# Gate-table products of a hybrid decoder step: the low part and the gate matching moved from GpSimd to VectorE

## The chip, the cores and the metric

One core of one Trainium2 chip runs one launch of the kernel. The metric is the device time of that launch in microseconds (us), the median of three runs. Engines are named as in the profile: PE is TensorE (PEld its weight loads), DVE is VectorE, ACT is ScalarE, POOL is GpSimd, SP issues most of the DMAs.

## What is computed

One decoder layer for 1024 prompt positions and 8 x 4 sample positions, 1056 columns in all. A token mixer (RWKV7 heads beside a pooling path) is followed by PEER, a lookup of 8 heads x 16 experts out of 16,384 per token, and by a gated embedding. The change lies in PEER:

```python
q = (xb @ wq).reshape(PEER_BLOCK, PEER_HEADS, 2, PEER_DK_HALF)
s1 = jnp.einsum('thc,nc->thn', q[:, :, 0], sub_keys[0])
s2 = jnp.einsum('thc,nc->thn', q[:, :, 1], sub_keys[1])
v1, i1 = lax.top_k(s1, PEER_TOPK)
v2, i2 = lax.top_k(s2, PEER_TOPK)
cand = (v1[..., :, None] + v2[..., None, :]).reshape(PEER_BLOCK, PEER_HEADS, PEER_TOPK * PEER_TOPK)
sc, ci = lax.top_k(cand, PEER_TOPK)
e1 = jnp.take_along_axis(i1, ci // PEER_TOPK, axis=-1)
e2 = jnp.take_along_axis(i2, ci % PEER_TOPK, axis=-1)
expert = e1 * N_KEYS + e2
gate = jax.nn.softmax(sc.astype(jnp.float32), axis=-1)
ue = jnp.take(u_tab, expert, axis=0)
act = jax.nn.gelu(jnp.einsum('thkd,td->thk', ue, xb).astype(jnp.float32), approximate=False) * gate
ve = jnp.take(v_tab, expert, axis=0)
return jnp.einsum('thk,thkd->td', act.astype(xb.dtype), ve)
```

## The kernel before

The 1056 columns are split in two. The last 384 gather their experts' rows (POOL's indirect DMAs). The first 672 are dense: every one of the 16,384 experts is computed for every column (U product, GELU, times a gate table, V product), and a table with one gate for each expert and column makes the unchosen ones zero. These tables are what the change touches.

The program has three stretches. First come the mixer's projections and most of the RWKV chunks. In the second, `phase_c` projects one group of 256 or 288 columns (W_out, then the queries) on PE, with weights that SP loads block by block (`whi`, `wlo` from `wc_d`), while `b_stream` runs the last RWKV chunks (small products at L470, with steps `ltm`, `lts`, `yx`, `yo` on POOL) and `t_stream` selects experts and builds gate tables for the group before. In the third, `dense` runs the expert products (L1118) on PE, block after block, and the gathers go on beside it.

The selection (`top`, `select`) takes the best 16 of each half and of their sums with DVE's eight-wide maximum, index and replace operations. Gates and codes come out in different orders, so they are matched: for two heads at a time `oh` is a 16 x 16 comparison of positions (L851, 512 columns), it is multiplied by the gates (L852), and summed along the row (L856). This is done four times for a tile of 128 columns, and once for the tile of 32 columns, which lies on the partitions as four sets of two heads.

The gate table of a token is a product of one-hot matrices over its 128 (head, rank) pairs, which lie on the partitions: row e1, column e2, weighted by the gate. The gate is split in two fp16 parts, high and low, in `e16` (fields 0 to 3 are e1, e2, the high part, the low part). For eight tokens at a time, in tile `ab` (fp16, two buffers), 84 times in all:

- L901 on DVE compares an iota with e1 and e2: two one-hot blocks, 2048 columns;
- L902 on DVE multiplies e2's block by the high part into a third block, 1024 columns;
- L904 multiplies e2's own block in place by the low part, in two halves of 512 columns. `GLO(t)` chooses the engine: POOL, unless t is a multiple of 12, which sends one half in three to DVE. The POOL operation goes through the helper `PTT`, so the profile shows it under L127;
- L912 on PE multiplies, for each token, the high block and the low block with e1's block (16 matmuls of 128 x 128), and ACT at L913 copies four tokens at a time to `gst`. Each 32 tokens are written to `g_d` by a DMA.

No table or cost of the program's author sets the order: the generators are merged by their share of steps, and the program's builder then schedules each engine's list by its own estimate. Each engine runs its list in order.

Of the kernel before, what the change touches and what calls it, by code (L numbers as in the profile page):

```python
# [16 lines left out]
ALU = mybir.AluOpType  # L17
# [30 lines left out]
GT8 = 8  # L48
SH = 4
NTC = ND // TC  # L50
EB = 128
# [12 lines left out]
def body(ctx, tc, io):  # L64
    nc = tc.nc
    mm = nc.tensor.matmul
    TT, STT, TS, ACT = (nc.vector.tensor_tensor, nc.vector.scalar_tensor_tensor, nc.vector.tensor_scalar,
                        nc.scalar.activation)
# [17 lines left out]
    def v3(ap, n):  # L86
        return ap.rearrange("p (a b) -> p a b", b=n)
# [38 lines left out]
    def PTT(out, a, b, op):  # L126
        nc.gpsimd.tensor_tensor(out, a, b, op=op)  # L127

    def PS(tag):
        return pools[tag].tile([128, 512], F32, name="ps", tag="bc" if tag in ("b0", "b1") else tag)  # L130
# [614 lines left out]
    def top(tk, pos, mt):  # L745
        src = sc_d[TIDX[pos]]
        if mt > TC:
            m, nh, loads = mt, HEADS, [(slice(0, mt), 0)]
        else:
            m, nh = mt * SH, HEADS // SH  # L750
            loads = [(slice(g * mt, (g + 1) * mt), 2 * nh * g) for g in range(SH)]
        V12 = tk.tile([128, HEADS, 2, TOPK], F32, name="V12", bufs=1)
        I12 = tk.tile([128, HEADS, 2, TOPK], U32, name="I12", bufs=1)
        for i in range(2 * nh):
            if i % 4 == 0:
                sq = tk.tile([128, 4, 128], F32, name="scq", bufs=2)
                for d, j in loads:
                    nc.sync.dma_start(sq[d], src[:mt, j + i:j + i + 4, :])
            s_ = sq[:m, i % 4, :]
            v8, i8 = V12[:m, i // 2, i % 2, :], I12[:m, i // 2, i % 2, :]  # L760
            nc.vector.max(v8[:, 0:8], s_)
            nc.vector.max_index(i8[:, 0:8], v8[:, 0:8], s_)
            s2 = tk.tile([128, 128], F32, name="s2", bufs=2)
            nc.vector.match_replace(s2[:m], v8[:, 0:8], s_, -BIG)
            nc.vector.max(v8[:, 8:16], s2[:m])
            nc.vector.max_index(i8[:, 8:16], v8[:, 8:16], s2[:m])
            yield
        yield from select(tk, pos, mt, m, nh, V12, I12)


    def select(tk, col, mt, m, nh, V12, I12):
# [7 lines left out]
        def pairs(src, dst, add):  # L779
            off = 0  # L780
            for a, b, w in SEG:
                k = b - a
                o = dst[:m, :nh, off:off + k * w]
                s1, s2_ = src[:m, :nh, 0, a:b], src[:m, :nh, 1, 0:w]
                if k == 1:
                    s1 = s1.to_broadcast([m, nh, w])
                elif w == 1:
                    s2_ = s2_.to_broadcast([m, nh, k])
                else:
                    o = o.rearrange("p h (k w) -> p h k w", w=w)  # L790
                    s1 = s1[:, :, :, None].to_broadcast([m, nh, k, w])
                    s2_ = s2_[:, :, None, :].to_broadcast([m, nh, k, w])
                add(o, s1, s2_, op=ALU.add)
                off += k * w
# [37 lines left out]
        gt = tk.tile([128, HEADS, TOPK], F32, name="gt")  # L832
# [15 lines left out]
        for h0 in range(0, nh, hb):  # L848
            hs, sh = slice(h0, h0 + hb), [m, hb, TOPK, TOPK]
            oh = tk.tile([128, hb, TOPK, TOPK], F32, name="oh", bufs=2)  # L850
            TT(oh[:m], cF[:m, hs, :, None].to_broadcast(sh), CF[:m, hs, None, :].to_broadcast(sh), op=ALU.is_equal)  # L851
            PTT(oh[:m], oh[:m], gt[:m, hs, None, :].to_broadcast(sh), op=ALU.mult)  # L852
            ohs.append((hs, oh))
            yield
        for hs, oh in ohs:
# [26 lines left out]
        m = mt  # L882
        nq = m // GT8
        e16 = gp.tile([128, 128 // GT8, 4, GT8], F16, name="e16")
# [5 lines left out]
        for t1 in range(0, m, TC):  # L890
            st = gp.tile([128, EB, TC], F32, name="gst", bufs=2)
            for t2 in range(0, TC, GT8):
                t = t1 + t2
                nb = GT8 // 2
                ab = gp.tile([128, 3 * nb, EB, 2], F16, name="ab", bufs=2)

                def pairs(j, n):
                    e = e16[:, t // GT8, j:j + n].rearrange("p j (a b) -> p (j a) b", b=2)
                    return e[:, :, None, :].to_broadcast([128, n * nb, EB, 2])

                TT(ab[:, 0:2 * nb], iota16[:, None, :, :].to_broadcast([128, 2 * nb, EB, 2]), pairs(0, 2), op=ALU.is_equal)  # L901
                TT(ab[:, 2 * nb:], ab[:, nb:2 * nb], pairs(2, 1), op=ALU.mult)  # L902
                for q in range(2):
                    GLO(t + 4 * q)(ab[:, nb + 2 * q:nb + 2 * q + 2], ab[:, nb + 2 * q:nb + 2 * q + 2],  # L904
                                   e16[:, t // GT8, 3:4, 4 * q:4 * q + 4].rearrange("p j (a b) -> p (j a) b", b=2)[:, :, None, :]
                                   .to_broadcast([128, 2, EB, 2]), op=ALU.mult)
                for q in range(0, GT8, 4):
                    ps = PS("b3")
                    for i in range(4):
                        a, o = divmod(q + i, 2)  # L910
                        for k in (2 * nb, nb):
                            mm(ps[:, i * 128:(i + 1) * 128], ab[:, k + a, :, o], ab[:, a, :, o], start=k > nb, stop=k == nb)  # L912
                    ACT(st[:, :, t2 + q:t2 + q + 4].rearrange("p e t -> p t e"), v3(ps, 128), AF.Copy, scale=1.0 / GS)  # L913
                yield
            nc.sync.dma_start(g_d[:, :, (col + t1 - GA) // TC].rearrange("g p e t -> p g e t"), st.rearrange("p (g e) t -> p g e t", e=GQ))
# [156 lines left out]
    TT(setsum, ident[:, 0:TC], ident[:, TC:2 * TC], op=ALU.add)  # L1072
    for g in range(2, SH):
        TT(setsum, setsum, ident[:, g * TC:(g + 1) * TC], op=ALU.add)

    def GLO(t):
        return PTT if t % 12 else TT

    def xsplit():
        return (dr.tile([128, KB, ND], F32R, name="XH"), dr.tile([128, KB, ND], F32R, name="XL"))  # L1080
# [137 lines left out]
    for col in range(0, GT, 128):  # L1218
        m = min(128, GT - col)
# [183 lines left out]
def program(arrays, extra=()):  # L1403
    nc = bacc.Bacc("TRN2", target_bir_lowering=False, num_devices=1)
    io = {k: nc.dram_tensor(k, v.shape, mybir.dt.from_np(v.dtype), kind="ExternalInput").ap()
          for k, v in arrays.items()}
    for k, s in list(OUTS.items()) + list(extra):
        io[k] = nc.dram_tensor(k, s, F32, kind="ExternalOutput").ap()
    with tile.TileContext(nc, schedule_with_timeline_sim=True) as tc, ExitStack() as ctx:
        body(ctx, tc, io)  # L1410
    return nc
# [15 lines left out]
```

## Time and profile before

| what | value |
|---|---|
| median of 3 runs | 3326.09 us (3318.22 to 3327.06) |
| the profiled execution, its own time | 3320.66 us |
| its span, first to last instruction | 3318.5 us |
| mean clock granted to PE | 0.968 of full speed |
| busy share of the span | PE 94%, PEld 90%, DVE 78%, POOL 51%, ACT 34% |
| instructions | 66499 |

A busy share is a mean over stretches with different limits. The 2.2 us between span and time are start and end of the launch.

### The profile page before, as it was taken

How to read it: one execution, taken by the hardware profiler on the slowest of the kernel's cores; microseconds unless marked ns; L12 is line 12 of the kernel's file. 1: busy time of each engine (PE TensorE's matmuls, PEld its weight loads, DVE VectorE, ACT ScalarE, POOL GpSimd, SP SyncE). 2: the span in 40 equal slices, each digit the busy share in tenths (PEclk: the TensorE clock that was granted, in tenths of full speed). 3: DMA queues.
4: the chain of work that ended last, by engine and by line, in shares of the span. 5: the costliest groups of instructions: out<-in, count | busy, mean ns of one | idle time of the engine just before them, and what ended most of it. 6: DMA issues, size and time to landing. Idle time of an engine off the chain costs nothing.

```text
span 3318.5 us, 66499 instructions
## 1 busy us (share of the span) xinstructions
PE 3129.6 (94%) x26777; PEld 3000.2 (90%) x26777; DVE 2576.9 (78%) x4930; ACT 1129.7 (34%) x1732; POOL 1705.2 (51%) x1366
## 2 busy tenths in 40 slices
PE   8998898987988888999999999999999999999997
PEld 7886787876877787999999999999999999999997
DVE  7775333469599888789888888888888888888966
ACT  6442423434454555432222122222222222212243
POOL 5212232235464465247666665666566666666534
PEclk9999899988998988999999999999999999999998
DMA  3325557855776987559999899999999989999833
GB/s 117 117 87 128 149 142 230 278 176 173 213 214 200 282 260 224 198 209 350 341 350 328 325 354 331 328 343 339 330 336 353 329 326 341 333 332 340 309 109 127
DMA packets 437333, 858.89 MB, mean 259 GB/s; under 512 B 108960, under 2 KB 232096, under 8 KB 432544
## 3 DMA queue, kind: packets, MB, share of 16 engines
q1 hardware_dynamic: 326432, 451.93, 41.6%
q0 software_dynamic: 110592, 402.70, 33.0%
q8 instruction: 210, 3.44, 0.4%
q14 instruction: 99, 0.81, 0.1%
HBM read 733.92 MB, written 120.60 MB: 258 GB/s over the span
## 4 chain that ended last, share of the span: by engine, by line
PE 75%; DVE 12%; DMA 5%; issue 2%; ACT 2%; POOL 2%; SPq 1%; ACTq 0%; DVEq 0%; POOLq 0%
PE pd L1118 58%; PE ps L470 5%; PE ps L219 4%; DVE ab L901 2%; PE ps L653 2%; PE ps L655 2%; PE ps L654 2%; PE ps L302 1%; DMA whi<-wc_d 1%; PE ps L912 1%; DVE ab L902 1%; POOL ab L127 1%; DMA scq<-sc_d 1%; DVE ab L904 1%; DMA sc_d<-scs 1%
## 5 line engine op out<-in xcount | busy, mean ns | idle before, releaser
L1227 POOL DMA_INDIRECT row<-v,idx x384 | 542.9, 1414 | 313.7 <-DVE po L1244 154.0
L1227 POOL DMA_INDIRECT row<-u,idx x384 | 543.7, 1416 | 282.8 <-DVE row L1235 123.0
L1094 ACT ACTIVATE ehi<-eraw 128x1024 fp32r<-128x1024 f32 x278 | 294.9, 1061 | 1109.3 <-PE pd L1118 999.9
L1118 PE MATMUL pd<-XH,elo 128*128 128x336 f32 x2176 | 513.8, 317 | 2.4 <-DVE elo L1096 2.2
L1118 PE MATMUL pd<-XL,ehi 128*128 128x336 f32 x2176 | 514.4, 317 | 0.0
L1118 PE MATMUL pd<-XH,ehi 128*128 128x336 f32 x2176 | 512.5, 316 | 0.7 <-ACT ehi L1094 0.7
L1118 PE MATMUL pd<-wh,ehi 128*128 128x336 f32 (+1 forms) x2112 | 504.0, 317 | 6.3 <-DVE tg L1308 6.3
L1118 PE MATMUL pd<-wh,elo 128*128 128x336 f32 (+1 forms) x2112 | 503.9, 317 | 0.0
L1118 PE MATMUL pd<-wl,ehi 128*128 128x336 f32 (+1 forms) x2112 | 502.7, 317 | 0.0
L1244 DVE SCALAR_TENSOR_TENSOR po<-row,act,po 128x1024 f32<-128x1024 f32 x381 | 488.5, 1282 | 6.6 <-DMA row<-v,idx 0.2
L1235 DVE SCALAR_TENSOR_TENSOR row<-row,xt 128x1024 f32<-128x1024 f32 x384 | 455.0, 1219 | 8.3 <-DMA row<-u,idx 8.3
L1096 DVE TENSOR_TENSOR elo<-eraw,ehi 128x1024 fp32r<-128x1024 f32 x256 | 318.5, 1244 | 73.8 <-ACT ehi L1094 63.2
L1118 PEld LDWEIGHTS pd<-XH,elo 128*128 128x128 f32 x2176 | 373.0, 188 | 3.1 <-DVE elo L1096 2.7
L1118 PEld LDWEIGHTS pd<-XH,ehi 128*128 128x128 f32 x2176 | 372.7, 189 | 1.2 <-ACT ehi L1094 0.9
L1118 PEld LDWEIGHTS pd<-XL,ehi 128*128 128x128 f32 x2176 | 371.4, 188 | 0.2
L1118 PEld LDWEIGHTS pd<-wh,ehi 128*128 128x128 f32 x2112 | 362.5, 188 | 7.1 <-issue 6.9
L1118 PEld LDWEIGHTS pd<-wl,ehi 128*128 128x128 f32 x2112 | 362.7, 188 | 0.0
L1118 PEld LDWEIGHTS pd<-wh,elo 128*128 128x128 f32 x2112 | 361.9, 188 | 0.2
L653 PE MATMUL ps<-hi,whi 128*128 128x256 f32 (+1 forms) x592 | 189.1, 321 | 46.0 <-DMA whi<-wc_d 24.2
L1187 DVE TENSOR_TENSOR OT<-pd,OT 128x672 f32<-128x672 f32 x120 | 102.9, 858 | 148.5 <-PE pd L1118 147.5
L127 POOL TENSOR_TENSOR ab<-ab,e 128x512 f16<-128x512 f16 x110 | 143.5, 1317 | 135.3 <-DVE ab L902 96.4
L913 ACT ACTIVATE gst<-ps 128x512 f32<-128x512 f32 x168 | 174.2, 1098 | 94.9 <-PE ps L912 89.9
(427 smaller groups left out, 5431.2 us busy)
## 6 DMA issues: line engine op xcount, KB each, us to landing
eraw<-uT SPq DMA_DIRECT2D x128, 512.0 KB
eraw<-vP SPq DMA_DIRECT2D x128, 512.0 KB
g_d<-gst SPq DMA_DIRECT2D x21, 2048.0 KB
gq<-g_d SPq DMA_DIRECT2D x32, 1344.0 KB
whi<-wc_d SPq DMA_DIRECT2D x108, 256.0 KB
wlo<-wc_d SPq DMA_DIRECT2D x108, 256.0 KB
fdc<-fd SPq DMA_DIRECT2D x16, 896.0 KB
wc_d<-whi SPq DMA_DIRECT2D x40, 256.0 KB
```

What stands on the lines that cost most here:

```text
L127: nc.gpsimd.tensor_tensor(out, a, b, op=op)
L219: mm(ps[:, :XW], s[:, k, :], x[:, k, a:b], start=first, stop=last)
L470: mm(o[hs], l[hs], r[hs], start=start, stop=stop)
L653: mm(ps[:, :n], whi[:, kk, :], xhi[:, k, :n], start=k == 0, stop=False)
L913: ACT(st[:, :, t2 + q:t2 + q + 4].rearrange("p e t -> p t e"), v3(ps, 128), AF.Copy, scale=1.0 / GS)
L1094: ACT(hi, raw, AF.Copy)
L1096: sub(lo, raw, hi.bitcast(F32), op=ALU.subtract)
L1118: mm(ps[:, a, :n], w_[:, k, :], x_[:, s:s + n], start=first, stop=last)
L1187: TT(halves(OT[db]), ps[:, :, :NH], halves(OT[db]), op=ALU.add)
L1227: nc.gpsimd.indirect_dma_start(out=r[:m], out_offset=None, in_=io[tab], in_offset=bass.IndirectOffsetOnAxis(ap=idx[:m, hh, k:k + 1], axis=0))
L1235: STT(r[:m], r[:m], 1.0, xt[:m], op0=ALU.mult, op1=ALU.mult, accum_out=pre[:m, k:k + 1])
L1244: STT(po[:m], r[:m], act[:m, k:k + 1], po[:m], op0=ALU.mult, op1=ALU.add)
```

## The change

All products of the one-hot blocks run on DVE. The low part's two halves become one operation of 1024 columns, at the new L903. The multiplication of the gate matching (L852) goes from POOL to DVE. The function that chose the engine is gone. Lines after L903 move up by 3, and those after L1069 by 6.

```diff
@@ -849,7 +849,7 @@
             TT(oh[:m], cF[:m, hs, :, None].to_broadcast(sh), CF[:m, hs, None, :].to_broadcast(sh), op=ALU.is_equal)
-            PTT(oh[:m], oh[:m], gt[:m, hs, None, :].to_broadcast(sh), op=ALU.mult)
+            TT(oh[:m], oh[:m], gt[:m, hs, None, :].to_broadcast(sh), op=ALU.mult)
@@ -900,10 +900,7 @@
                 TT(ab[:, 0:2 * nb], iota16[:, None, :, :].to_broadcast([128, 2 * nb, EB, 2]), pairs(0, 2), op=ALU.is_equal)
                 TT(ab[:, 2 * nb:], ab[:, nb:2 * nb], pairs(2, 1), op=ALU.mult)
-                for q in range(2):
-                    GLO(t + 4 * q)(ab[:, nb + 2 * q:nb + 2 * q + 2], ab[:, nb + 2 * q:nb + 2 * q + 2],
-                                   e16[:, t // GT8, 3:4, 4 * q:4 * q + 4].rearrange("p j (a b) -> p (j a) b", b=2)[:, :, None, :]
-                                   .to_broadcast([128, 2, EB, 2]), op=ALU.mult)
+                TT(ab[:, nb:2 * nb], ab[:, nb:2 * nb], pairs(3, 1), op=ALU.mult)
                 for q in range(0, GT8, 4):
@@ -1072,9 +1069,6 @@
-    def GLO(t):
-        return PTT if t % 12 else TT
```

On POOL, in the stretch where the tables of the third tile are built, the list before has the products of `ab` between the steps of two RWKV chunks (a number behind a name counts copies of a tile):

```order
L127 TENSOR_TENSOR yx<-ltm,ident_103 128x256
L127 TENSOR_TENSOR ab<-ab,e_10302 128x512
L127 TENSOR_TENSOR ltm<-lts,nmt 128x256
L127 TENSOR_TENSOR ab<-ab,e_10302 128x512 x2
L127 TENSOR_TENSOR ltm<-lts,nmt 128x256
L127 TENSOR_TENSOR ab<-ab,e_10302 128x512
L127 TENSOR_TENSOR lts<-lts,s_10983 128x256
L127 TENSOR_TENSOR ab<-ab,e_10302 128x512
L127 TENSOR_TENSOR yo<-yo,fdc 128x256
L127 TENSOR_TENSOR ab<-ab,e_10302 128x512 x2
```

At the same place now:

```order
L127 TENSOR_TENSOR yx<-ltm,ident_103 128x256
L127 TENSOR_TENSOR ltm<-lts,nmt 128x256
L127 TENSOR_TENSOR lts<-lts,s_10952 128x256
L127 TENSOR_TENSOR ltm<-lts,nmt 128x256
L127 TENSOR_TENSOR yo<-yo,fdc 128x256
L127 TENSOR_TENSOR ltm<-lts,nmt 128x256 x2
L127 TENSOR_TENSOR lo<-y,hi 128x256 x4
```

The products of `ab` are gone from POOL's list and the RWKV steps stand behind each other.

On DVE, for the same tile, the list before:

```order
L902 TENSOR_TENSOR ab<-ab,e_10302 128x1024
L901 TENSOR_TENSOR ab<-iota_5647,e_10302 128x2048
L902 TENSOR_TENSOR ab<-ab,e_10302 128x1024
L904 TENSOR_TENSOR ab<-ab,e_10302 128x512
L901 TENSOR_TENSOR ab<-iota_5647,e_10302 128x2048 x2
L902 TENSOR_TENSOR ab<-ab,e_10302 128x1024 x2
L904 TENSOR_TENSOR ab<-ab,e_10302 128x512
L492 TENSOR_TENSOR lp<-ps,mask_101 128x512
```

And now:

```order
L603 TENSOR_REDUCE s_10945<-ps 128x4
L902 TENSOR_TENSOR ab<-ab,e_10286 128x1024
L604 TENSOR_SCALAR s_10945<-s_10945 128x4
L903 TENSOR_TENSOR ab<-ab,e_10286 128x1024
L606 TENSOR_TENSOR lts<-ps,s_10945 128x256
L610 TENSOR_REDUCE s_10952<-wn 128x4
L901 TENSOR_TENSOR ab<-iota_5647,e_10286 128x2048
L179 RECIPROCAL s_10952<-s_10952 128x4
L902 TENSOR_TENSOR ab<-ab,e_10286 128x1024
L903 TENSOR_TENSOR ab<-ab,e_10286 128x1024
L901 TENSOR_TENSOR ab<-iota_5647,e_10286 128x2048
```

Each group of eight tokens now has three wide operations on DVE. Before, two of three groups had two wide ones and a narrow one there with the other half on POOL, and the third group had two wide ones there with both halves on POOL.

## Rows read from the trace of the kernel before

**Rows 1.** The page, busy time of each engine, share of the span and number of instructions.
```profile
PE 3129.6 (94%) x26777; PEld 3000.2 (90%) x26777; DVE 2576.9 (78%) x4930; ACT 1129.7 (34%) x1732; POOL 1705.2 (51%) x1366
```

**Rows 2.** The view by stretches of the span: busy time of each engine (and number of instructions), clock granted to PE, DMA share, GB/s. The three stretches of the program, and the first 65 us of the second.
```profile
core 0: us, PE busy (x) PEld busy (x) DVE busy (x) ACT busy (x) POOL busy (x), PEclk, DMA share, GB/s
0.00:755.00 755.00, 673.00 (x8205) 602.24 (x8207) 400.54 (x882) 301.39 (x605) 209.97 (x243) 0.95 0.51 157
755.00:1335.00 580.00, 497.35 (x5885) 444.45 (x5882) 492.72 (x1671) 302.10 (x481) 306.46 (x286) 0.90 0.73 224
1335.00:3318.50 1983.50, 1959.28 (x12692) 1953.55 (x12692) 1683.64 (x2378) 526.20 (x647) 1188.74 (x838) 0.99 0.85 308
...
755.00:820.00 65.00, 50.39 (x623) 42.80 (x620) 64.97 (x224) 31.85 (x56) 39.45 (x41) 0.78 0.57 168
```

**Rows 3.** The chain that ended last, in the stretch from 755 to 1335 us: its shares by line (cut at the right by the view).
```profile
by line: DVE ab L901 11.9%; PE ps L470 6.9%; DMA whi<-wc_d 6.0%; PE ps L912 5.9%; DVE ab L902 5.1%; issue 4.6%; POOL ab L127 4.6%; PE ps L653 4.2%; DVE ab L904 3.8%; PE ps L655 3.8%; PE ps L654 3.6%; DMA wlo<-wc_d 2.7%; DVE h L710 2.3%; ACT
```

**Rows 4.** Who waited for whom from 755 to 1335 us: us in total, times, the longest in us.
```profile
PE ps L653 <- DMA whi<-wc_d: 24.2, 8, 5.3
PE ps L912 <- DVE ab L902: 13.1, 9, 6.4
PE ps L912 <- POOL ab L127: 9.4, 15, 1.3
PE ps L912 <- DVE ab L904: 8.0, 9, 1.6
DVE ab L901 <- PE ps L912: 18.6, 16, 4.9
DVE ab L901 <- POOL ltm L127: 1.6, 1, 1.6
POOL ab L127 <- DVE ab L902: 96.4, 40, 7.3
POOL ltm L127 <- PE ps L470: 30.1, 8, 16.4
```

**Rows 5.** Groups of instructions from 755 to 1335 us, shapes apart: number, busy us, mean ns of one, and the idle time before them with what ended it.
```profile
L901 DVE TENSOR_TENSOR ab<-iota,e 128x2048 f16<-128x2048 f16 x84 | 127.7, 1526 | 22.7 <-PE ps L912 18.6 <-ACT e L887 2.3 <-POOL ltm L127 1.6
L902 DVE TENSOR_TENSOR ab<-ab,e 128x1024 f16<-128x1024 f16 x84 | 69.4, 833 | 0.8
L904 DVE TENSOR_TENSOR ab<-ab,e 128x512 f16<-128x512 f16 x58 | 46.1, 802 | 0.4
L851 DVE TENSOR_TENSOR oh<-cF,CF 128x512 f32<-128x512 f32 x21 | 19.6, 950 | 0.0
L127 POOL TENSOR_TENSOR ab<-ab,e 128x512 f16<-128x512 f16 x110 | 143.5, 1317 | 135.3 <-DVE ab L902 96.4 <-PE ps L912 12.2 <-DVE SC L810 7.4
L127 POOL TENSOR_TENSOR ltm<-lts,nmt 128x256 f32<-128x256 f32 x30 | 29.9, 1004 | 38.2 <-PE ps L470 30.1 <-ACT lts L498 7.9
L127 POOL TENSOR_TENSOR oh<-oh,gt 128x512 f32<-128x512 f32 x21 | 29.2, 1394 | 17.7 <-DVE oh L851 17.7
```

**Rows 6.** The same lines: number, shortest, median and longest duration in ns, first and last start in us. L851 and the POOL product of `oh` of the whole span have 33; the first row on L851 is of the second stretch, the last two are of 1335 to 1460 us.
```profile
L901 DVE TENSOR_TENSOR ab<-iota,e x84: 1200/1226/2946, 761.6 to 1320.9; 128x2048 f16<-128x2048 f16 x84
L902 DVE TENSOR_TENSOR ab<-ab,e x84: 640/684/2774, 765.9 to 1323.1; 128x1024 f16<-128x1024 f16 x84
L904 DVE TENSOR_TENSOR ab<-ab,e x58: 400/758/2233, 775.1 to 1323.8; 128x512 f16<-128x512 f16 x58
L127 POOL TENSOR_TENSOR ab<-ab,e x110: 1036/1187/4007, 766.7 to 1323.9; 128x512 f16<-128x512 f16 x110
L851 DVE TENSOR_TENSOR oh<-cF,CF x21: 665/685/1760, 798.6 to 1297.3; 128x512 f32<-128x512 f32 x21
L851 DVE TENSOR_TENSOR oh<-cF,CF x8: 665/678/693, 1404.3 to 1451.9; 128x512 f32<-128x512 f32 x8
L127 POOL TENSOR_TENSOR oh<-oh,gt x8: 1287/1644/2278, 1405.0 to 1453.7; 128x512 f32<-128x512 f32 x8
```

**Rows 7.** The instructions in order of time on DVE from 926 to 950 us: start us, us, engine, line, operation, number, and idle time before with its releaser.
```profile
932.25 3.17 DVE L901 TENSOR_TENSOR ab<-iota,e 128x2048 f16<-128x2048 f16 x2 [1.64 <-POOL ltm L127]
...
938.92 1.85 DVE L901 TENSOR_TENSOR ab<-iota,e 128x2048 f16<-128x2048 f16 x1 [0.52 <-PE ps L912]
...
943.31 1.21 DVE L901 TENSOR_TENSOR ab<-iota,e 128x2048 f16<-128x2048 f16 x1
...
945.71 2.06 DVE L901 TENSOR_TENSOR ab<-iota,e 128x2048 f16<-128x2048 f16 x1
```

**Rows 8.** The same view on POOL, same time.
```profile
926.63 2.25 POOL L127 TENSOR_TENSOR yo<-yo,fdc 128x256 f32<-128x256 f32 x1 [2.35 <-DVE yo L617]
...
932.16 1.04 POOL L127 TENSOR_TENSOR ab<-ab,e 128x512 f16<-128x512 f16 x1
936.19 3.51 POOL L127 TENSOR_TENSOR ab<-ab,e 128x512 f16<-128x512 f16 x3 [2.99 <-DVE ab L902]
939.75 1.62 POOL L127 TENSOR_TENSOR ltm<-lts,nmt 128x256 f32<-128x256 f32 x1
...
945.62 1.06 POOL L127 TENSOR_TENSOR ab<-ab,e 128x512 f16<-128x512 f16 x1 [2.52 <-PE ps L470]
946.65 4.42 POOL L127 TENSOR_TENSOR lo<-y,hi 128x256 fp32r<-128x256 f32 x4
```

**Rows 9.** The chain that ended last, in order of time, after 1335 us: the longest pieces.
```profile
1366.60 653.85 PE pd L1118 x4256
2021.32 575.96 PE pd L1118 x3746
2598.15 559.15 PE pd L1118 x3640
```

## The prediction

> **What bounds the kernel now.** I read the busy shares first. PE has 94% and DVE 78% [rows 1], but a mean over three stretches says little, so the view by stretches came next [rows 2]. From 1335 us to the end PE is busy 1959.28 of 1983.5 us, and the longest pieces of the chain are nothing but expert products [rows 9]. That stretch begins when the second one is done and lasts as long as its matmuls do. What happens on DVE or POOL there costs nothing while PE stays full, and a microsecond saved before 1335 us is a microsecond saved at the end.
>
> The change lies in the second stretch, 755 to 1335 us. There no engine is full: DVE 492.72 of 580 us, PE 497.35, POOL 306.46, and PE gets a clock of only 0.90 [rows 2]. In its first 65 us DVE is busy 64.97 us [rows 2]; so DVE is the nearest to a bound. The chain through the stretch [rows 3] is a patchwork: the gate tables' operations on DVE (L901 11.9%, L902 5.1%, L904 3.8%), POOL's half products of `ab` 4.6%, table matmuls 5.9%, and weight loads 6.0 + 2.7%. In us of 580: 69.0, 29.6, 22.0, 26.7, 34.2 and 50.5. The waits [rows 4] show the ring behind it: PE waits for `ab` (13.1 + 9.4 + 8.0 = 30.5 us), DVE's L901 waits for PE to free one of the two `ab` buffers (18.6 us), and POOL waits 96.4 us for L902 with its other work queued behind the waiting product. Part of those 96.4 us cost nothing, since POOL is not the bound. But `ltm` and `lo` stand behind such a wait in POOL's list.
>
> **What DVE pays now.** L901 has a median of 1226 ns and a mean of 1526; L902 684 and 833; L904 a shortest of 400 and a mean of 802; L851 685 and 950 [rows 5, 6]. The excess comes from POOL. At 945.62 us POOL starts a product of `ab` that lasts 1.06 us; DVE's L901 starts at 945.71 and lasts 2.06 us, 0.85 us longer than the free one of 1.21 us at 943.31 [rows 7, 8]. The other way round it holds too: POOL's `yo` at 926.63 took 2.25 us while DVE was at work, against a mean of 1.004 us for an `ltm` of the same size [rows 5, 8]. The two engines hold each other up, and whichever starts second pays.
>
> **The change part by part**, from 755 to 1335 us.
>
> *Low part.* Removed: 110 POOL products of 1317 ns (143.5 us of POOL) and 58 DVE halves (46.1 us). Added: 84 DVE products of 1024 columns. The trace has the same shape in L902, on the same tile: 684 ns free, 833 ns at today's mean. That is 57.5 to 70.0 us, so DVE's own part grows by 11.4 to 23.9 us.
>
> *Gate matching.* Removed: 21 POOL products of 1394 ns (29.2 us). Added: 21 DVE products of 512 f32 columns; L851 has that shape and type, 685 to 950 ns, so 14.4 to 19.9 us. Eight of each more come after 1335 us [rows 6] and cost 8 x 0.678 = 5.4 us of DVE beside a full PE [rows 2]: nothing at the end, and those 5.4 us if the chain there should leave PE. The four that are left of 33 lie before 755 us and are priced with the 21's error.
>
> *Holds that go.* If no DVE operation of these lines were held any more, they would take 84 x (1.226 + 0.684 + 0.684) + 42 x 0.685 = 246.7 us. If all stayed at today's means: 84 x (1.526 + 0.833 + 0.833) + 42 x 0.950 = 308.0 us. Today they take 127.7 + 69.4 + 46.1 + 19.6 = 262.8 us. So DVE's bill lies between -16.1 and +45.2 us. The moved products are 172.7 of POOL's 306.46 us, 56%; if holds went in that proportion, DVE would pay 246.7 + 0.44 x 61.3 = 273.7 us, +10.9. But these products come just while DVE works on the same tile, so they make more of the collisions than their share: in the stretch shown each of the three held L901 (the pair at 932.25, those at 938.92 and 945.71) began while a POOL `ab` was at work, and the free one at 943.31 did not [rows 7, 8]. With three quarters of the holds gone it is 262.0 us, -0.8. I take **0** for DVE's own time.
>
> *Hand-overs.* This is where the gain is. POOL's products are 26.7 us of the chain, some 20 pieces of 1.317 us. Each is replaced by half of a wide DVE product, 0.342 us: 20 x 0.342 = 6.8 us. That is -19.9 us. From DVE's side: it stood 18.6 + 1.6 = 20.2 us before L901 for a buffer or for POOL [rows 4], and with the POOL leg out of the ring most of that closes. The two readings are one gain seen twice, so I do not add them. Some of it stays, since the ring still runs through PE and ACT: I take **-18 us**. Below, the bound is 0, if something of nearly equal length takes the place at once (weight loads); above, 26.7 us with the products free, and the 16.1 us of holds: -43.
>
> *POOL's other work.* `ltm`, `lts`, `yo`, `lo` lose what stood before them in the list. POOL is not the bound and its own pieces on the chain are small apart from `ab`; I put it at 0. No DMA is added, removed or moved by hand. The builder reorders SP's and PE's lists slightly around it, which I can't price and leave to the range.
>
> **The sum.** 3320.66 - 18 = 3302.7 us on the scale of the profiled execution. The median of the three runs is 5.4 us above that execution, so 3308 us for a median: 0.5% faster. A difference under 0.3%, some 10 us, can't be told from none with this kernel, whose runs before spread over 9 us.
>
> **The rivals.**
>
> *DVE becomes the bound: slower.* In the first 65 us of the stretch DVE already has no free time, and after the change it carries three wide operations for each group of tokens and twice the `oh` work. If the remaining POOL work (`ltm`, `elo`, `lo`, `sa`) steps into the freed time and holds DVE as often as now, the bill is between +10.9 and +45.2 us, middle 28; at DVE's share of 492.72 / 580 = 0.85 that is +24 us, and no gain comes from hand-overs, since DVE is never free to use them: 3350 us. It decides if the mean of L901 after the change stays above some 1.4 us and DVE's idle time in the stretch falls under 40 us without the stretch getting shorter. For it: DVE is the fullest engine in that first piece, and its shortest possible bill is only 16.1 us under today's. Against it: 172.7 of POOL's 306.46 us leave, and with them the holds seen in [rows 7, 8]. The Trainium skill's page "Perfetto Trace Analysis", section "Optimizing Scalar/DVE Operations", speaks for this rival: with a saturated DVE it may make sense to offload to GpSimd, which is what the change undoes; the same passage warns that the shared port may eat the gain. By the advice the time would be that of this rival; the rows bear out the warning more than the advice, hence a chance of one in five.
>
> *Absorbed by the weights: no change.* PE's longest wait in the stretch is for `whi` (24.2 us), and weight loads are 50.5 us of the chain. A load can start only when PE has freed a buffer, so a quicker gate table lets PE arrive earlier at the same load and wait there. If three quarters of the 18 us go that way, -4 us remain: 3322 us. For it: the chain changes between these paths every few us. Against it: a PE that gets through earlier also frees the buffers earlier.
>
> **How the numbers follow.** The forecast (hand-overs go, DVE even) gets 0.57, with its own range from 3283 (the -43) to 3316; the slower rival 0.21; no change 0.22. So faster 0.57, same 0.22, slower 0.21. The range for 8 in 10 goes from 3283 to 3340, which leaves out the upper half of the slower rival and a little below.
>
> **What would show it.** Right: no `ab` and no `oh` product on POOL; POOL busy about 173 us less in the stretch; the mean of L901 at 1.25 to 1.35 us, of L902 and L903 at 0.68 to 0.75; L901's wait for PE down by half or more; the stretch ending near 1317 us with PE's clock above 0.90; the last stretch unchanged at some 1983 us. Wrong: L901's mean still at 1.4 or more, now beside `ltm`, `lo` and `elo`; DVE full over the stretch; PE's wait for L903 longer than the 30.5 us for the three lines before; or a stretch that ends where it did, with PE's wait for `whi` grown by what the tables lost. My sum would be wrong in kind if the last stretch changed its length, since I hold that nothing there depends on the moved work.

## The result, and the profile after

The kernel after takes a median of 3303.9 us (3300.53 to 3310.19, 6 runs), against 3323.7 us (3318.22 to 3327.06, 6 runs) before: a ratio of 0.9943, interval 0.9931 to 0.9955. It is 19.8 us faster. The forecast of 3308 us, faster, held, and the time lies inside the range. The steps behind it held only in part; the rest of the text is on that.

The profiled execution of after took 3310.19 us, the longest of its six, and that of before 3320.66 us. So the trace shows some 10 of the 20 us, and differences of a few us between traces are read with care below; the times of the runs decide.

The page of after, the line of busy times, to be set beside [rows 1]:

```profile
PE 3115.4 (94%) x26777; PEld 2995.7 (91%) x26777; DVE 2561.4 (77%) x4989; ACT 1127.6 (34%) x1734; POOL 1509.4 (46%) x1223
```

The view by stretches, columns as in [rows 2]:

```profile
0.00:755.00 755.00, 673.20 (x8241) 601.50 (x8242) 402.92 (x891) 301.62 (x607) 205.40 (x240) 0.95 0.52 157
755.00:1335.00 580.00, 494.31 (x5924) 450.93 (x5922) 474.31 (x1713) 303.20 (x488) 135.91 (x157) 0.90 0.76 230
1335.00:3308.50 1973.50, 1947.92 (x12616) 1943.22 (x12615) 1684.15 (x2386) 522.83 (x641) 1168.11 (x828) 0.99 0.85 307
```

POOL fell by 170.6 us in the second stretch, as the 172.7 us of moved products say. DVE, which took the work over, is busy 18.4 us *less* there. PE's clock stayed at 0.90.

The groups from 755 to 1335 us, columns as in [rows 5]:

```profile
L901 DVE TENSOR_TENSOR ab<-iota,e 128x2048 f16<-128x2048 f16 x84 | 103.5, 1238 | 50.1 <-PE ps L909 49.8
L902 DVE TENSOR_TENSOR ab<-ab,e 128x1024 f16<-128x1024 f16 x84 | 65.3, 784 | 0.6
L903 DVE TENSOR_TENSOR ab<-ab,e 128x1024 f16<-128x1024 f16 x84 | 61.1, 733 | 0.6
L851 DVE TENSOR_TENSOR oh<-cF,CF 128x512 f32<-128x512 f32 x21 | 14.9, 745 | 1.0 <-ACT cF L828 0.9
L852 DVE TENSOR_TENSOR oh<-oh,gt 128x512 f32<-128x512 f32 x21 | 15.5, 759 | 0.0
L710 DVE SCALAR_TENSOR_TENSOR h<-h,vecs,rstd 128x256 f32<-128x256 f32 x24 | 16.8, 770 | 2.0 <-DMA hT_d<-h 2.0
```

L901 is down from 1526 to 1238 ns, where its median is 1224: nearly nothing holds it now. L902 fell from 833 to 784. The new L903 costs 733 ns, less than two of the shortest halves before (400 ns each). Together the five lines of `ab` and `oh` take 260.3 us, against 262.8 before. L710, which the change does not touch, fell as well; before, it was:

```profile
L710 DVE SCALAR_TENSOR_TENSOR h<-h,vecs,rstd 128x256 f32<-128x256 f32 x24 | 20.5, 924 | 0.0
```

DVE from 926 to 936 us, columns as in [rows 7]; none of these is a long one:

```profile
928.20 1.23 DVE L901 TENSOR_TENSOR ab<-iota,e 128x2048 f16<-128x2048 f16 x1 [1.18 <-PE ps L909]
929.46 0.69 DVE L902 TENSOR_TENSOR ab<-ab,e 128x1024 f16<-128x1024 f16 x1
930.46 1.22 DVE L901 TENSOR_TENSOR ab<-iota,e 128x2048 f16<-128x2048 f16 x1 [0.31 <-PE ps L909]
931.61 0.69 DVE L903 TENSOR_TENSOR ab<-ab,e 128x1024 f16<-128x1024 f16 x1
```

The waits from 755 to 1335 us, columns as in [rows 4]:

```profile
DVE ab L901 <- PE ps L909: 49.8, 33, 7.4
PE ps L653 <- DMA whi<-wc_d: 21.1, 9, 4.9
PE ps L909 <- DVE ab L902: 19.6, 5, 8.9
PE ps L909 <- ACT gst L910: 12.7, 24, 1.9
PE ps L909 <- DVE ab L903: 3.7, 5, 1.3
```

PE waits for `ab` 23.3 us (19.6 + 3.7) instead of 30.5. L901's own wait for PE, though, did not shrink: it grew from 18.6 to 49.8 us. DVE reaches it sooner and stands there. And the chain through the stretch, as in [rows 3]:

```profile
by line: DMA whi<-wc_d 10.5%; PE ps L470 10.3%; PE ps L909 9.2%; PE ps L653 5.9%; PE ps L655 5.5%; PE ps L654 4.8%; DMA wlo<-wc_d 3.8%; PE pd L1112 3.3%; DVE ab L901 3.0%; DMA sc_d<-scs 2.4%; PE ps L739 2.4%; ACT gst L910 2.3%; DVE h L710 2
```

DVE's L901 went from 11.9% to 3.0% and POOL's `ab` is gone; weight loads (10.5 + 3.8%, before 6.0 + 2.7%) and PE's own matmuls came in their place.

**Which mark carries the end.** The prediction took 1335 us, the last table matmul, for the start of the full-PE stretch. The chain gives a sharper mark. In order of time (start us, us, what), before and then after, around the last score matmuls (L739, the end of the last group's `phase_c`):

```profile
1360.61 4.87 PE pd L1118 x20
1365.48 1.11 PE ps L739 x10
1366.60 33.41 PE pd L1118 x217
```

```profile
1350.69 5.96 PE pd L1112 x20
1356.64 1.11 PE ps L739 x10
1357.76 42.33 PE pd L1112 x275
```

From the last L739 on, the chain is expert products with hardly a gap: before, PE is busy for all of the 1790.70 us from there to 3157 us, and only the last 161 us have steps of other engines on the chain. The start of the last L739 is read from its line (number, shortest/median/longest ns, first and last start; before, after):

```profile
L739 PE MATMUL ps<-keys,q x288: 270/275/421, 606.8 to 1366.3; 128*128 128x128 f32 x128, 128*32 128x128 f32 x16
L739 PE MATMUL ps<-keys,q x288: 270/275/421, 606.3 to 1357.5; 128*128 128x128 f32 x128, 128*32 128x128 f32 x16
```

From there to the end of the span it is 3318.5 - 1366.3 = 1952.2 us before and 3308.5 - 1357.5 = 1951.0 after. In all but one of the kernels below it is 1951 to 1955 us. So nearly the whole difference is made before the last L739, and what the change is worth is how much sooner PE gets there.

### The profile page after: what moved, and what is told of

It is laid out like the page before. It is cut to its first block, busy times and chain, and to the rows that moved or that the text cites. A ratio compares the mean times of both kernels' runs of the same rounds, so it can differ in the third digit from the quotient of the medians.

```text
span 3308.5 us, 66279 instructions
## 1 busy us (share of the span) xinstructions
PE 3115.4 (94%) x26777; PEld 2995.7 (91%) x26777; DVE 2561.4 (77%) x4989; ACT 1127.6 (34%) x1734; POOL 1509.4 (46%) x1223
## 4 chain that ended last, share of the span: by engine, by line
PE 77%; DVE 9%; DMA 8%; ACT 2%; issue 2%; POOL 1%; SPq 1%; ACTq 0%; DVEq 0%; POOLq 0%
PE pd L1112 58%; PE ps L470 5%; PE ps L219 4%; PE ps L653 2%; PE ps L655 2%; PE ps L654 2%; DMA whi<-wc_d 2%; PE ps L909 2%; PE ps L302 1%; DMA scq<-sc_d 1%; DMA sc_d<-scs 1%; DMA wlo<-wc_d 1%; DMA hT_d<-h 1%; PE ps L739 1%; DVE I L762 1%
## 5 line engine op out<-in xcount | busy, mean ns | idle before, releaser
L653 PE MATMUL ps<-hi,whi 128*128 128x256 f32 (+1 forms) x592 | 189.3, 322 | 48.7 <-DMA whi<-wc_d 21.1
L127 POOL TENSOR_TENSOR ltm<-lts,nmt 128x256 f32<-128x256 f32 x98 | 82.1, 846 | 311.8 <-PE ps L470 189.0
L910 ACT ACTIVATE gst<-ps 128x512 f32<-128x512 f32 x168 | 169.5, 1110 | 67.1 <-PE ps L909 62.0
```

The lines of the kernel that those rows point to most:

```text
L653: mm(ps[:, :n], whi[:, kk, :], xhi[:, k, :n], start=k == 0, stop=False)
```

## The experiments

All are built on the kernel after, unless said. Times are medians, ratios are to the kernel before on the same chip (medians of 3322.68 to 3324.45 us there). "Over after" is the difference of a ratio to 0.9943, times 3323 us; its error adds both intervals in quadrature and is 5 to 7 us. A trace is one execution, which can lie some us off the median: that of `hold`, for one, took 3322.59 us, 6.5 us above its median.

Some edits add lines, and numbers move: in `handover`, `hold`, `queue` and `hold_free`, L905 is the comparison (L901), L906 the product with the high part (L902), L907 (L908 in `handover`) that with the low part (L903), and L917 the table matmuls (L909).

### One part of the change alone

`low_only`, on the kernel after:

```diff
-            TT(oh[:m], oh[:m], gt[:m, hs, None, :].to_broadcast(sh), op=ALU.mult)
+            PTT(oh[:m], oh[:m], gt[:m, hs, None, :].to_broadcast(sh), op=ALU.mult)
```

> Only the low part's product moves to VectorE (one operation of 1024 columns); the gate matching's product stays on GpSimd. Both theories of the gain (holds taken away, hand-overs taken away) put it here: 110 of the 131 products that leave GpSimd in the second stretch, and 143.5 of the 172.7 us. Expected 16 to 22 us under the kernel before, L901's mean on VectorE at 1.22 to 1.28 us. If the reordering of the lists made the gain, this kernel may stand anywhere within 10 us of the one before.

`oh_only`: the same line on the kernel before, from `PTT` to `TT`.

> Only the gate matching's product moves to VectorE; two of three halves of the low part stay on GpSimd as before. VectorE gets 21 x 0.68 = 14 us more work in the stretch and is relieved of 29.2 us of GpSimd products. Expected within 6 us of the kernel before, either way; L901's mean still near 1.5 us. A gain of 10 us or more would say that the matching carries the change.

Measured: `low_only` 3302.11 us, 0.9933 (0.9921 to 0.9946). `oh_only` 3325.05 us, 1.0005 (0.9996 to 1.0015). The first is not to be told from after, the second not from before. The low part carries the change; the gate matching alone is worth nothing measurable.

L901 from 755 to 1335 us, of `low_only` and of `oh_only`:

```profile
L901 DVE TENSOR_TENSOR ab<-iota,e 128x2048 f16<-128x2048 f16 x84 | 115.4, 1379 | 36.7 <-PE ps L909 35.4 <-ACT e L887 1.2
L901 DVE TENSOR_TENSOR ab<-iota,e 128x2048 f16<-128x2048 f16 x84 | 118.8, 1421 | 25.8 <-PE ps L912 16.1 <-POOL ab L127 3.1 <-ACT e L887 2.0
```

Here both expectations missed: 1.22 to 1.28 us was expected for `low_only`, near 1.5 for `oh_only`. `low_only` has the whole gain with L901 still held (1379 ns), and `oh_only` has none of it with L901 held less than before (1421 against 1526). So the holds on L901 alone do not say what a kernel takes.

### A hand-over without the work

`handover`: DVE multiplies all but 16 of the low part's 1024 columns. These 16 are two products of 8 columns, which go to POOL or DVE as the halves did before the change: 110 POOL products, for which PE's tables wait. (In this and the next three cuts, `low(...)` is a helper that picks the low gates; its definition and that of `GLO` are left out here.)

```diff
-                TT(ab[:, nb:2 * nb], ab[:, nb:2 * nb], pairs(3, 1), op=ALU.mult)
+                EL = EB - 2
+                TT(ab[:, nb:2 * nb, 0:EL, :], ab[:, nb:2 * nb, 0:EL, :], low(0, nb, EL), op=ALU.mult)
+                for q in range(2):
+                    GLO(t + 4 * q)(ab[:, nb + 2 * q:nb + 2 * q + 2, EL:, :], ab[:, nb + 2 * q:nb + 2 * q + 2, EL:, :],
+                                   low(2 * q, 2 * q + 2, 2), op=ALU.mult)
```

> As after, but VectorE's low product leaves out the last 2 of the 128 rows of each block, and the 110 halves that GpSimd had before are GpSimd operations of 8 columns on just these rows (VectorE has the other 58 of 8 columns). So the tables still wait for GpSimd in the same 110 places, and GpSimd is busy for a fraction of a microsecond each time. If holds made the gain: within 5 us of the kernel after, some 3300 to 3310, with L901's mean on VectorE under 1.3 us. If hand-overs made it (my term of 18 us): the gain is gone, 3318 or more.

Measured: 3313.33 us, 0.9975 (0.9964 to 0.9985), 11 us over after. Its groups from 755 to 1335 us:

```profile
L905 DVE TENSOR_TENSOR ab<-iota,e 128x2048 f16<-128x2048 f16 x84 | 109.5, 1309 | 29.3 <-PE ps L917 27.5 <-POOL ab L127 1.4
L910 DVE TENSOR_TENSOR ab<-ab,e 128x8 f16<-128x8 f16 x58 | 13.7, 235 | 0.0
L127 POOL TENSOR_TENSOR ab<-ab,e 128x8 f16<-128x8 f16 x110 | 47.6, 442 | 209.3 <-DVE ab L906 161.2 <-PE ps L917 17.2 <-DVE K L820 11.6
```

POOL's work on `ab` is a third of what it was (47.6 us against 143.5), the first operation on DVE is held only a little (1309 ns), and half of the gain is lost all the same. Not all of it is the hand-over: DVE has 13.7 us of small products of its own (the halves that go to DVE, L910). What that makes is priced below. Nor does the trace show PE waiting for POOL: its waits for `ab` from DVE are 17.2 + 5.7 us, as in after, and for POOL's piece it waits hardly at all:

```profile
PE ps L917 <- POOL ab L127: 0.3, 1, 0.3
```

This execution and the one traced of after differ by only 1.5 us (3311.7 and 3310.19), so where the 11 us of the medians lie stays open.

### The work without a hand-over

`hold`: POOL multiplies the third block, L902's result, by the low part into a tile `dm` that nobody reads, at the same places. It waits for L902's operation, but no table waits for it; only the next writer of the same `ab` buffer does.

```diff
+                for q in range(2):
+                    if (t + 4 * q) % 12:
+                        dm = gp.tile([128, 2, EB, 2], F16, name="dm", bufs=1)
+                        PTT(dm, ab[:, 2 * nb + 2 * q:2 * nb + 2 * q + 2], low(2 * q, 2 * q + 2, EB), op=ALU.mult)
```

> As after, with 110 GpSimd products of 128 x 512 added whose result nobody reads: they read the third block of ab and the low gates, as many and as wide as the ones that the change took away. No table waits for them; only the ab buffer's next writer does, as it waits for TensorE anyway. If holds made the gain: it is gone, 3318 or more, with L901's mean back at 1.4 us or more. If hand-overs made it: as after, 3300 to 3310, whatever L901's mean.

`queue`: the same with 8 columns, so that POOL's list is blocked by the same waits and hardly works.

```diff
+                        dm = gp.tile([128, 2, 2, 2], F16, name="dm", bufs=1)
+                        PTT(dm, ab[:, 2 * nb + 2 * q:2 * nb + 2 * q + 2, EB - 2:, :], low(2 * q, 2 * q + 2, 2), op=ALU.mult)
```

> As after, with 110 GpSimd products of only 8 columns whose result nobody reads, each reading the end of the block that L902 writes. So GpSimd's list waits for L902 in 110 places, as before the change, and its other work (ltm, lts, yo, lo) queues behind; but no table waits for GpSimd and VectorE is held for a small time only. The run named handover lost some 12 of the 20 us. If the list behind the waiting product was what cost them: 8 to 14 us over the kernel after, some 3312. If it was the tables' own wait for GpSimd: within 4 us of after, some 3304.

`hold_free`: the 512 columns again, but read from the iota, so that a product waits for nothing in the ring either.

```diff
+                        dm = gp.tile([128, 2, EB, 2], F16, name="dm", bufs=1)
+                        PTT(dm, iota16[:, None, :, :].to_broadcast([128, 2, EB, 2]), low(2 * q, 2 * q + 2, EB), op=ALU.mult)
```

> As after, with 110 GpSimd products of 128 x 512 added that read only the iota and the gates, so they wait for no VectorE operation and nobody waits for them. What they bring is GpSimd's time and the holds on VectorE. If holds by themselves cost time: 8 us or more over after, with VectorE's means of L901 and L902 up by 0.1 us or more. If only the waits in GpSimd's list and the hand-over cost: within 4 us of after.

Measured: `hold` 3316.06 us, 0.9979 (0.9970 to 0.9989), 12 us over after; `queue` 3306.85, 0.9952 (0.9938 to 0.9967), 3 us over after and not to be told from it; `hold_free` 3335.53, 1.0037 (1.0023 to 1.0052), 31 us over after and 12 us over *before*. Groups from 755 to 1335 us, of `hold`, of `queue`, of `hold_free`:

```profile
L905 DVE TENSOR_TENSOR ab<-iota,e 128x2048 f16<-128x2048 f16 x84 | 120.3, 1438 | 18.2 <-PE ps L917 15.7 <-ACT e L887 2.5
L907 DVE TENSOR_TENSOR ab<-ab,e 128x1024 f16<-128x1024 f16 x82 | 84.7, 1039 | 0.6
L127 POOL TENSOR_TENSOR dm<-ab,e 128x512 f16<-128x512 f16 x108 | 151.2, 1400 | 163.9 <-DVE ab L906 151.4 <-DVE SC L810 6.2 <-DVE K L820 2.6
```

```profile
L905 DVE TENSOR_TENSOR ab<-iota,e 128x2048 f16<-128x2048 f16 x84 | 104.3, 1247 | 45.4 <-PE ps L917 30.1 <-POOL elo L127 7.4 <-issue 5.5
L127 POOL TENSOR_TENSOR dm<-ab,e 128x8 f16<-128x8 f16 x110 | 59.1, 537 | 233.7 <-DVE ab L906 220.6 <-DVE s L604 3.8 <-DVE SC L810 3.2
```

```profile
L905 DVE TENSOR_TENSOR ab<-iota,e 128x2048 f16<-128x2048 f16 x83 | 117.9, 1426 | 21.5 <-PE ps L917 21.5
L906 DVE TENSOR_TENSOR ab<-ab,e 128x1024 f16<-128x1024 f16 x83 | 74.4, 904 | 0.8
L907 DVE TENSOR_TENSOR ab<-ab,e 128x1024 f16<-128x1024 f16 x81 | 70.2, 873 | 0.8
L127 POOL TENSOR_TENSOR dm<-iota,e 128x512 f16<-128x512 f16 x110 | 149.4, 1358 | 35.8 <-DVE e L889 29.6
```

In `hold` the low product on DVE (L907) takes 1039 ns instead of 733, the compare 1438 instead of 1238: POOL runs beside them and holds them. The trace also shows where that reaches PE, whose waits for `ab` are 39.7 us against 23.3 in after:

```profile
PE ps L917 <- DVE ab L907: 20.9, 19, 2.5
PE ps L917 <- DVE ab L906: 18.8, 14, 6.6
```

In `queue`, where POOL waits longer (220.6 us) but is soon done, DVE runs free (1247) and the time stays. So a blocked list on POOL costs little here, and POOL's work costs some 12 us with no table waiting for the product. The Trainium skill's page "SBUF — State Buffer", section "Who interferes with whom", states that a VectorE instruction with two inputs in SBUF contends with a GpSimd instruction that reads SBUF; these rows agree, with 1426 and 1438 ns beside POOL's products against 1238.

`hold_free` holds DVE no more than `hold` (1426 against 1438, 873 against 1039) and yet costs 19 us more. A part of its POOL timeline (columns as in [rows 8]) shows what else is new:

```profile
900.06 12.11 POOL L127 TENSOR_TENSOR dm<-iota,e 128x512 f16<-128x512 f16 x8
912.13 2.85 POOL L127 TENSOR_TENSOR ltm<-lts,nmt 128x256 f32<-128x256 f32 x2
```

The products come in runs now, and steps of an RWKV chunk stand behind 12 us of them. That this makes the 19 us is argued; no run separates it.

### What a microsecond of DVE is worth

`no_low` leaves out the multiplication by the low part (the tables then count e2's block itself in place of the gate's low half). It says what the 84 products cost where they stand now.

```diff
-                TT(ab[:, nb:2 * nb], ab[:, nb:2 * nb], pairs(3, 1), op=ALU.mult)
```

> As after, without the low part's product: e2's block stays as the comparison left it, so the low half of the gates is left out of the computation (TensorE still multiplies the block). VectorE loses 84 operations, 61 us of the 468 in the stretch. If VectorE still bounds the stretch after the change: 25 us or more under after. If it is no longer the bound, and TensorE's list and the weight loads are: under 10 us less than after.

Measured: 3283.16 us, 0.9887 (0.9870 to 0.9904), 19 us under after. The operations left out took 61.1 us there, so by this run a microsecond of DVE in this stretch is worth some 0.30 us at the end (0.2 to 0.4 by the intervals). Put to `hold` and `handover`, by the view by stretches (in this order):

```profile
755.00:1335.00 580.00, 481.86 (x5852) 435.19 (x5853) 526.21 (x1688) 293.97 (x476) 286.22 (x262) 0.91 0.75 224
...
755.00:1335.00 580.00, 491.94 (x5918) 444.75 (x5913) 486.58 (x1778) 302.08 (x487) 187.39 (x265) 0.91 0.76 231
```

In `hold` DVE is busy 526.21 us against 474.31, 51.9 more; times 0.30 it is 16 us, and 12 were measured. In `handover` it is 12.3 more, 4 us of the 11 measured; some 7 us are left for the hand-over itself, little more than the error of 5. The same sum for `hold_free` (511.85 us of DVE, +37.5) gives 11 us where 31 were measured, the gap named above. Its stretch runs on past 1335 us; over the whole execution its DVE is 54.9 us busier than after's (2616.3 and 2561.4), which gives 16 us and still leaves a gap of 15.

The price is rough. By it the change's own 18.4 us of DVE are worth 5.5 of the 20 us. And it does not order the kernels: `all_pool`, below, has less DVE time in the stretch than after (466.37 us) and takes some 15 us more; `low_lo`, below, has more (500.93) and takes 25 us less. POOL's busy time there sorts them better, though coarsely: the five kernels with 279 us or more (before, `oh_only`, `hold`, `hold_free`, `all_pool`), which all have 108 or more POOL products of 512 fp16 columns in the tables' loop, take 3316 us or more, and the nine with under 200 us take 3313 or less.

### The other way, and the width

`all_pool`, on the kernel before: every half of the low part on POOL, DVE freed of its 58.

```diff
     def GLO(t):
-        return PTT if t % 12 else TT
+        return PTT
```

> The other way: as before, but every half of the low part on GpSimd, 168 instead of 110 (the matching's product there too). GpSimd gets 58 x 1.3 = 76 us more in the stretch, VectorE 46 us less. If what counts is VectorE's own work: faster than before by up to 10 us. If holds and the tables' wait for GpSimd count: slower, by 58/110 of the 20 us that taking the 110 away brought, so 10 us over before or more, with L901's mean over 1.55 us.

`dve_halves`, on after: L903 as two products of 512 columns on DVE.

```diff
-                TT(ab[:, nb:2 * nb], ab[:, nb:2 * nb], pairs(3, 1), op=ALU.mult)
+                for q in range(2):
+                    TT(ab[:, nb + 2 * q:nb + 2 * q + 2], ab[:, nb + 2 * q:nb + 2 * q + 2],
+                       ..., op=ALU.mult)
```

> As after, with the low part in two VectorE operations of 512 columns instead of one of 1024. The trace of before had 400 ns for the shortest half, so 84 x (2 x 0.41 - 0.68) = 12 us more VectorE time. The run without the low product took 61 us from VectorE and gave 19 us, so 12 us should cost some 4: 0 to 6 us over after. 10 us or more would say that the width, and not the engine, made the gain.

Measured: `all_pool` 3320.3 us, 0.9989 (0.9980 to 0.9997). A loss was expected and there is none; it is just under before. The profiled execution was the longest of its twelve (3329.67 us). Its second stretch:

```profile
755.00:1335.00 580.00, 499.75 (x5846) 441.60 (x5846) 466.37 (x1587) 295.81 (x477) 375.93 (x343) 0.90 0.74 223
```

DVE is busy 26.4 us less than before, worth 8 us by the 0.30, and 4 were measured; L901's mean is 1507 ns, not over 1550 as expected for a loss. PE's wait for POOL's `ab` rose from 9.4 to 15.3 us. One reading is that relief on DVE and longer waits for POOL cancel in part; no run separates them. It means that the price is not in proportion to the number of products on POOL: moving the last third there costs nothing, taking all away gains 20 us.

`dve_halves` 3299.77 us, 0.9927 (0.9915 to 0.9940), not to be told from after. Its halves take 75.1 us where L903 takes 61.1:

```profile
L904 DVE TENSOR_TENSOR ab<-ab,e 128x512 f16<-128x512 f16 x168 | 75.1, 489 | 0.6
```

Fourteen us more on DVE should by the 0.30 cost 4; the measured difference is -5 with an error of 6. The single wide operation is not what made the kernel faster.

### Further in the same direction

`lo_dve`: the subtraction for the low half of `phase_c`'s input moves from POOL to DVE. `both_dve`: that, and the low parts `elo` of the first expert blocks and the last query blocks too. `low_lo`: `lo_dve` with the gate matching back on POOL, as in `low_only`.

```diff
-            PTT(lo[:, k, :n], src, hi[:, k, :n].bitcast(F32), op=ALU.subtract)
+            TT(lo[:, k, :n], src, hi[:, k, :n].bitcast(F32), op=ALU.subtract)
```

> As after, and the subtraction that splits activations for the projections (lo, 48 operations of 256 and 288 columns, 32 of them in the stretch at 0.81 to 0.89 us on GpSimd) on VectorE too, where an operation of 256 f32 columns takes 0.41 us. It takes away the holds on L710 (mean 0.770 us, 0.47 free: 7 us) for 13 us of VectorE work, and a hand-over ahead of TensorE's matmuls. If holds and hand-overs are worth more than VectorE's time, 3 to 10 us under after; if VectorE's time counts, as much over it.

> As lo_dve, and the subtraction elo of the first expert blocks and of the last query blocks (11 operations of 1024 f32 columns in the stretch, 2.73 us each on GpSimd, where they hold L902 for some 5 us) on VectorE, at 1.23 us each. VectorE gets 13.5 us more and is relieved of the holds; TensorE's expert blocks wait 1.5 us less each. Expected within 5 us of lo_dve, either way.

> The two moves that gained, without the one that did not: the low part and the activations' lo on VectorE, the matching's product back on GpSimd. Holds by the matching (29 us of GpSimd in the stretch) come back, 14 us of VectorE work go. Expected at lo_dve's time within 4 us; the fastest of the kernels if the matching's move costs the few us that low_only and after differ by (3302 and 3304).

Measured: `lo_dve` 3299.16 us, 0.9927 (0.9912 to 0.9942); `both_dve` 3304.5, 0.9941 (0.9929 to 0.9953); `low_lo` 3279.81, 0.9869 (0.9854 to 0.9883). The first two are not to be told from after. `both_dve` is the one kernel whose last stretch grew: 3300.3 - 1321.1 = 1979.2 us from the last L739, 28 us more than after, so most of the 36 us by which it comes there earlier is given back.

`low_lo` is the fastest of all, 44 us under before and 25 under after, and 19 us faster than `lo_dve`, where no difference beyond 4 was expected. Its line L739, its second stretch, and two of its groups there:

```profile
L739 PE MATMUL ps<-keys,q x288: 270/275/421, 603.0 to 1320.4; 128*128 128x128 f32 x128, 128*32 128x128 f32 x16
```

```profile
755.00:1335.00 580.00, 509.25 (x6141) 466.98 (x6139) 500.93 (x1776) 314.89 (x508) 147.00 (x146) 0.93 0.80 246
```

```profile
L901 DVE TENSOR_TENSOR ab<-iota,e 128x2048 f16<-128x2048 f16 x84 | 112.2, 1340 | 19.0 <-PE ps L909 19.0
L680 DVE TENSOR_TENSOR lo<-h,hi 128x256 fp32r<-128x256 f32 x24 | 9.1, 430 | 0.0
```

PE comes to the last L739 at 1320.4 us, 37 earlier than after; a part of that may be the execution, the shortest of its four, against the longest of six for after. L901 waits 19.0 us for PE (`lo_dve` 37.3), though it is held more (1340 ns; `lo_dve` 1278). Why the gate matching on POOL is worth 19 us here and nothing in `low_only` stays open: the builder orders every engine's list anew with each edit, and no run held the order fixed. So the order of the lists is a rival for a part of the 20 us of the change as well. Against it as the whole cause speaks that all nine kernels without the 108 or more POOL products of 512 fp16 columns, each with lists of its own, are faster than before by 8 us or more.

## Why the prediction was right, and where not

- **DVE's own bill: right.** It was put at 0, between -16.1 and +45.2; it is 260.3 - 262.8 = -2.5 us. The guess that three quarters of the holds go is near the truth: of the 61.3 us between all holds and none, 13.6 are left (260.3 - 246.7). L901's mean of 1238 ns lies just under the 1.25 to 1.35 us given; L903's 733 is in its bounds and L902's 784 a little over.
- **Hand-overs, -18 us: right as a total, not as a cause.** This is the step that did not hold. The whole gain was put on hand-overs and none on holds. In the runs, hand-overs with next to no work cost 11 us (`handover`), of which some 7 are left for the hand-over itself, with an error of 5; the same small products with no table waiting cost 3 (`queue`). Work without a hand-over costs 12 (`hold`), but there DVE is 51.9 us busier than after, since it does the whole low product too; before, it was 18.4 us busier, worth 5.5 us at the 0.30. So hand-overs and DVE's time explain some 12 of the 20 us, and the rest is not attributed. That the sum came within 2 us of the result is in part luck. The prediction argued that DVE's bill stays even, so holds are worth nothing; but DVE took 84 x 1024 columns over at that even bill only because the holds went, and it lost some more on lines that are not touched, such as L710 (20.5 to 16.8 us). They had to be priced as work that DVE would have paid for otherwise.
- **"L901's wait for PE down by half": wrong.** It went from 18.6 to 49.8 us. With the POOL leg out of the ring, DVE is early and waits for PE's list, which has the other streams in it. What fell was PE's wait for `ab` (30.5 to 23.3), and the work of L901 and of POOL on the chain (11.9 + 4.6% to 3.0%).
- **PE's clock above 0.90: not so**, it is 0.90 as before.
- **The stretch ends near 1317 us; the last one unchanged: right, by two marks.** The last table matmul starts at 1332.5 us before and at 1318.8 after. From the last L739 it is 1952.2 and 1951.0 us. L739 itself came 8.8 us earlier in an execution that was 10.5 us shorter.
- **Gate matching: right** at about nothing (`oh_only` +0.05%, interval -0.04 to +0.15%). Beside `lo` on DVE it is not nothing (`low_lo`), for a reason that stays open.
- **The rival "DVE becomes the bound": no.** It was to be seen by a mean of L901 above 1.4 us; it is 1.238, and DVE's busy time fell. `hold_free` shows the state that this rival meant (1426 ns, slower than before), but it takes POOL work that the change had removed. The Trainium skill's page "Perfetto Trace Analysis", section "Optimizing Scalar/DVE Operations", says that offloading a saturated DVE to GpSimd may make sense, and warns that between these two it might not help, since they share a port. Here DVE was busy for 85% of the stretch and not saturated, and taking the offload back gained 0.57%; that agrees with the warning.
- **The rival "absorbed by the weights": in part.** Weight loads rose from 8.7 to 14.3% of the chain, but PE's wait for `whi` fell (24.2 to 21.1 us).

## What to carry to other kernels

Before moving elementwise work between DVE and POOL, price three things apart: the work, the holds on what DVE runs beside it (lines that the edit does not touch, too), and the step in the ring that waits for it. Runs with a tiny product at the same place, and with the full product that nobody reads, help to tell the last two apart, but each also moves DVE's time and the order of the lists, so compare several such kernels before a sum is made of them. And find the operation after which the chain is nearly one engine alone (here the last L739, a constant 1952 us from the end): the start of that operation, not the end of a stage, says what an edit before it is worth.

## What the hardware showed that was not expected

In this kernel, POOL products that nobody waits for and that wait for nothing cost more than those that they stand for: `hold_free`, with its 110 idle products of 512 columns, is 12 us slower than the kernel before, in which POOL's 110 products are on the tables' path. The order of POOL's list differs too, so this is not a price of the engines alone.

A tiny POOL product is not always cheap beside a busy DVE. Those of 8 columns have a mean of 442 ns in `handover`, and this is their line (shortest/median/longest ns):

```profile
L127 POOL TENSOR_TENSOR ab<-ab,e x110: 193/204/1909, 767.0 to 1309.2; 128x8 f16<-128x8 f16 x110
```

Half of them take about 0.2 us; the rest take up to 1.9. One that starts at 791.60 us takes 0.73 us, beside a low product on DVE (L908) that started at 791.58 and took 0.67.
